# A sum of reciprocals on one core: the first load made in two transfers of 64 partitions

## The chip, the core and the metric

The kernel runs on one core of a Trainium2 chip. The metric is the device time of one execution in microseconds, as the median of several runs. Lower is better.

## What is computed

The input has 32 x 512 rows of 1024 values in float32, all positive. Of each row the kernel gives the sum of the reciprocals.

```python
def setup_inputs():
    batch, seq, dim = 32, 512, 1024
    return {
        "x": np.abs(np.random.randn(batch, seq, dim)).astype(np.float32) + 1e-6,
    }

def reference(x: np.ndarray) -> np.ndarray:
    return np.sum(1.0 / x, axis=-1).astype(np.float32)
```

The input is 64 MiB, the output 64 KiB. Each of the 128 partitions of on-chip memory gets 128 rows of the 16,384, and what the text calls "a row" is such a row on all partitions at once: 128 x 1024 values, 512 KiB.

## The kernel before

The rows pass through a ring of 40 places in on-chip memory. A plan, written out as a list of short words, gives the order of all operations. `D4 D8 D15 D13` at its start are loads of 4, 8, 15 and 13 rows, which fill the ring; the later loads, each smaller than these in the end, refill the places that have been used up.

The reciprocal is not taken directly. For the two halves a and b of a row, 1/a + 1/b = (a + b) / (ab). So the product ab is formed on GpSimd (`P`) or VectorE (`V`, `W`), ScalarE takes its logarithm (`L`) and the exponential of minus that (`E`), and VectorE multiplies and sums (`R`). The sum a + b comes from TensorE, as two matrix products with the identity that accumulate (`S`); in other rows VectorE multiplies both halves with 1/(ab) and sums. TensorE also copies halves of some rows into its accumulator memory for VectorE (`C`).

A load, a product on GpSimd and a copy on TensorE:

```python
            if op == "D":
                n, r = r, loaded
                while n:
                    q, at, w = place(r)
                    a = q % R
                    m = min(n, R - a, LAST - r) if r < LAST else 1
                    inst = nc.sync.dma_start(
                        out=ring[:, a : a + m, at : at + 2 * w],
                        in_=x_v[:, q : q + m, at : at + 2 * w],
                    )
                    note("SP", inst, writes=rows(r, m))
                    r, n = r + m, n - m
                loaded = r
            elif op == "P":
                # ... (cut)
                    inst = nc.gpsimd.tensor_tensor(
                        out=prod[:, p : p + m, :w],
                        in0=ring[:, a : a + m, at : at + w],
                        in1=ring[:, a : a + m, at + w : at + 2 * w],
                        op=mult,
                    )
                    note("POOL", inst, rows(r, m), slots(r, m))
                # ... (cut)
            elif op == "C":
                copied[r] = b
                inst = nc.tensor.matmul(
                    ps[:, b, : place(r)[2]],
                    lhsT=ident,
                    rhs=xs(r, 1),
                    start=True,
                    stop=True,
                )
                note("PE", inst, rows(r, 1, 1), [("bank", b)])
```

`x_v[:, q : q + m, ...]` has 128 partitions, and each partition's m rows lie one after the other in memory: four rows are 16 KiB in a piece.

`note` keeps account of what has read and written each place, and declares a dependency unneeded where another wait already implies it:

```python
    def note(engine, inst, reads=(), writes=()):
        # ... (cut: collects in `needed` the operations that this one must follow)
        for other in needed:
            o_inst, o_engine, o_tick, _, _, o_known = other
            if o_engine == engine:
                continue
            if o_tick <= known.get(o_engine, 0):
                tc.declare_no_dep(inst, o_inst, reason="implied by other waits")
                continue
            for e, t in o_known.items():
                known[e] = max(known.get(e, 0), t)
            known[o_engine] = max(known.get(o_engine, 0), o_tick)
        # ... (cut: a load is entered under a name of its own, "load 1", "load 2", ...)
```

Of the kernel before, what the change touches and what calls it, by code (L numbers as in the profile page):

```python
# [11 lines left out]
def kernel(  # L12
# [5 lines left out]
    nc = tc.nc  # L18
    f32 = mybir.dt.float32
    P = 128  # L20
# [58 lines left out]
    x_v = x.flatten_outer_dims().rearrange("(p f) d -> p f d", p=P)  # L79
# [16 lines left out]
    ring = pool.tile([P, R, D], f32)  # L96
# [15 lines left out]
    def place(r):  # L112
        if r < LAST:
            return r, 0, H
        part, q = divmod(r - LAST, F - LAST)
        return LAST + q, part * H, H // 2

    def xs(r, h):
        q, at, w = place(r)
        return ring[:, q % R, at + h * w : at + (h + 1) * w]  # L120

    loaded = 0
# [10 lines left out]
    def note(engine, inst, reads=(), writes=()):  # L133
        inst = inst.ins
        known = dict(begun.get(engine, {}))
        before = {}
        for spaces, writing in ((reads, False), (writes, True)):
            for space in spaces:
                for other in history.get(space, ()):
                    if writing or other[3]:  # L140
                        before[other[0].name] = other
        needed = sorted(before.values(), key=lambda o: -o[4])
# [4 lines that stand above are left out]
            if o_tick <= known.get(o_engine, 0):  # L147
                tc.declare_no_dep(inst, o_inst, reason="implied by other waits")
                continue
            for e, t in o_known.items():  # L150
                known[e] = max(known.get(e, 0), t)
            known[o_engine] = max(known.get(o_engine, 0), o_tick)
        count[engine] = count.get(engine, 0) + 1
        begun[engine] = known
        entry = (engine, count[engine])
        if engine == "SP":
            entry = (f"load {count[engine]}", 1)
        for spaces, writing in ((reads, False), (writes, True)):
            for space in spaces:
                history.setdefault(space, []).append(  # L160
                    (inst, *entry, writing, sum(count.values()), known)
                )

    def rows(r, n, h=None):
        spaces = []
        for q, at, w in (place(i) for i in range(r, r + n)):
            end = at + 2 * w
            if h is not None:
                at, end = at + h * w, at + (h + 1) * w
            spaces += [("row", q % R, i) for i in range(at, end, H // 2)]  # L170
        return spaces

    def slots(r, n):
        return [("slot", pslot[q]) for q in range(r, r + n)]

    with tc.manual_schedule():
        for op, r, n, b in ops:
            p = pslot.get(r)
# [3 lines that stand above are left out]
                    q, at, w = place(r)  # L182
                    a = q % R
                    m = min(n, R - a, LAST - r) if r < LAST else 1
                    inst = nc.sync.dma_start(  # L185
                        out=ring[:, a : a + m, at : at + 2 * w],
                        in_=x_v[:, q : q + m, at : at + 2 * w],
                    )
                    note("SP", inst, writes=rows(r, m))
                    r, n = r + m, n - m  # L190
                loaded = r
            elif op == "P":
                while n:
                    q, at, w = place(r)
                    a, p = q % R, pslot[r]
                    m = min(n, R - a)
# [18 lines that stand above are left out]
            elif op in "WV":  # L215
                w = place(r)[2]
                in1 = xs(r, 1) if op == "W" else ps[:, copied[r], :w]
                inst = nc.vector.tensor_tensor(  # L218
                    out=prod[:, p, :w], in0=xs(r, 0), in1=in1, op=mult
                )  # L220
                if op == "W":
                    read = rows(r, 1)
                else:
                    read = rows(r, 1, 0) + [("bank", copied[r])]
                note("DVE", inst, read, slots(r, 1))
            elif op == "S":
                bank[r] = b
                halves.add(r)
                for h in range(2):
# [3 lines that stand above are left out]
                        rhs=xs(r, h),  # L233
                        start=h == 0,
                        stop=h == 1,
                    )
                    note("PE", inst, rows(r, 1, h), [("bank", b)])
            elif op == "L":
                pg = prod[:, p : p + n, : place(r)[2]]
                inst = nc.scalar.activation(out=pg, in_=pg, func=Ln, scale=S)  # L240
                note("ACT", inst, writes=slots(r, n))
            elif op == "E":
                pg = prod[:, p : p + n, : place(r)[2]]
                rc = pg
                if b is not None:
                    rc = ps[:, b : b + n, : place(r)[2]]
                    for j in range(n):
                        bank[r + j] = b + j
                inst = nc.scalar.activation(out=rc, in_=pg, func=Exp, scale=-1.0)  # L249
                if b is None:  # L250
                    note("ACT", inst, writes=slots(r, n))
                else:
                    banks = [("bank", b + j) for j in range(n)]
                    note("ACT", inst, slots(r, n), banks)
            elif op == "R":
                q, at, w = place(r)
                other = ps[:, bank[r], :w]
                if r in halves:
                    row = prod[:, p, :w]
                else:  # L260
                    row = ring[:, q % R, at : at + 2 * w]
                    row = row.rearrange("p (h e) -> p h e", h=2)
                    other = other.unsqueeze(1).to_broadcast([P, 2, w])
                total = sums[:, q : q + 1]
                inst = nc.vector.tensor_tensor_reduce(  # L265
                    out=row,
                    in0=row,
                    in1=other,
                    scale=S,
                    scalar=total if q in summed else 0.0,  # L270
                    op0=mult,
                    op1=add,
                    accum_out=total,
                )
                summed.add(q)
                note(
                    "DVE",
                    inst,
                    [("bank", bank[r])],
                    slots(r, 1) if r in halves else rows(r, 1),  # L280
                )
        nc.sync.dma_start(out=out_v, in_=sums)
# [30 lines left out]
```

## Time and profile before

| | |
|---|---|
| time, median of 3 | 169.06 us (168.96 to 169.12) |
| span of the profiled execution | 167.1 us |
| read from HBM | 67.11 MB, 402 GB/s over the span |
| load queue | 94.8% of 16 DMA engines' span |
| busy: PE, DVE, ACT, POOL | 135.1, 128.2, 133.0, 128.0 us |
| the first load | 2048 KB; issued at 0.74 us, landed 7.3 us later |

The span is what the profiler saw from the first instruction to the last. PE is TensorE, DVE VectorE, ACT ScalarE, POOL GpSimd, and SP SyncE, which issues the loads. A line such as L197 is a line of the kernel. Where a group is listed with what "waited" before it, the arrow names the operation whose completion ended the wait. The DMA share is the mean busy share of the 16 DMA engines; it can exceed 1 in a short stretch, since a packet counts where it starts.

### The profile page before, as it was taken

Reading aid. Unit: us, or ns where it says so; the run is one execution under the profiler, and the core shown is the slowest. Engines: PE = TensorE matmul, PEld = TensorE weight load, DVE = VectorE, ACT = ScalarE, POOL = GpSimd, SP = SyncE. Lnnn points to the kernel's source line nnn. Section 1 sums busy time; section 2 is a strip of 40 time slices with the busy share of each in tenths; the row PEclk is TensorE's granted clock in tenths of the full one; section 3 lists DMA queues with packets and bytes.
Section 4 is the critical chain, followed back from the end, with each engine's and each line's share of the span. In section 5 each row is a group of like instructions: output and inputs, shape, how many; then the busy total and the mean of one; then the engine's idle time right before and its main releaser. Section 6 shows DMA issues by size and latency. Waiting matters only on the chain.

```text
span 167.1 us, 1335 instructions
## 1 busy us (share of the span) xinstructions
PE 135.1 (81%) x292; PEld 55.7 (33%) x292; DVE 128.2 (77%) x283; ACT 133.0 (80%) x161; POOL 128.0 (77%) x80
## 2 busy tenths in 40 slices
PE   0092799039999999977998999999699669989692
PEld 0030343023444334323333434434244133424261
DVE  0010298604789989886798898799999999999994
ACT  3045159207999999977999997999899999999992
POOL 1070792039999999939999997966899997979970
PEclk9999599965999999999999999999999999999999
DMA  5998999999999998999998989999999999999910
GB/s 192 435 502 377 471 471 471 471 408 408 408 408 407 439 466 377 441 424 439 412 471 384 479 377 447 416 449 412 422 428 429 405 432 408 428 408 409 396 64 16
DMA packets 4760, 67.26 MB, mean 403 GB/s; under 512 B 528, under 2 KB 656, under 8 KB 2192
## 3 DMA queue, kind: packets, MB, share of 16 engines
q1 hardware_dynamic: 4752, 67.18, 94.8%
q8 instruction: 2, 0.03, 0.1%
q14 instruction: 6, 0.05, 0.1%
HBM read 67.11 MB, written 0.07 MB: 402 GB/s over the span
## 4 chain that ended last, share of the span: by engine, by line
DMA 60%; DVE 16%; PE 15%; issue 3%; ACT 2%; SPq 1%; DVEq 0%; ACTq 0%
DMA ring<-in_x_dram 60%; PE ps L230 11%; DVE ring L265 10%; DVE prod L265 4%; PE ps L207 4%; DVE prod L218 2%; ACT prod L240 1%; DVE sums L265 1%; ACT prod L249 1%; ACT ps L249 1%; SPq L185 1%; DVEq L308 0%; ACTq L240 0%
## 5 line engine op out<-in xcount | busy, mean ns | idle before, releaser
L197 POOL TENSOR_TENSOR prod<-ring 128x1024 f32<-128x1024 f32 (+2 forms) x74 | 127.3, 1752 | 33.6 <-DMA ring<-in_x_dram 31.6
L230 PE MATMUL ps<-ring,ident 128*128 128x512 f32 (+1 forms) x260 | 118.6, 605 | 4.3 <-DVE sums L265 3.1
L240 ACT ACTIVATE prod<-prod 128x1024 f32<-128x1024 f32 (+2 forms) x80 | 69.0, 876 | 27.0 <-POOL prod L197 26.2
L265 DVE CUSTOM_DVE_ANT_1 ring<-ring,ps 128x1024 f32<-128x1024 f32 (+1 forms) x65 | 76.3, 1209 | 8.4 <-ACT ps L249 8.4
L230 PEld LDWEIGHTS ps<-ring,ident 128*128 128x128 f32 x260 | 49.8, 197 | 72.7 <-issue 51.7
L265 DVE CUSTOM_DVE_ANT_0 prod<-prod,ps 128x512 f32<-128x512 f32 (+1 forms) x63 | 40.7, 678 | 1.4 <-ACT prod L249 1.3
L207 PE MATMUL ps<-ring,ident 128*128 128x512 f32 x32 | 19.9, 712 | 24.5 <-DMA ring<-in_x_dram 24.5
L249 ACT ACTIVATE ps<-prod 128x1024 f32<-128x1024 f32 (+2 forms) x40 | 33.9, 854 | 2.5 <-DVE sums L265 1.8
L249 ACT ACTIVATE prod<-prod 128x1024 f32<-128x1024 f32 (+2 forms) x40 | 34.6, 874 | 0.8
L218 DVE TENSOR_TENSOR prod<-ring,ps 128x512 f32<-128x512 f32 x16 | 10.9, 685 | 26.6 <-PE ps L207 26.4
L207 PEld LDWEIGHTS ps<-ring,ident 128*128 128x128 f32 x32 | 5.9, 212 | 35.1 <-issue 16.3
L265 DVE DVE_READ_ACCUMULATOR2_ANT sums<- 128x1 f32 x130 | 10.7, 82 | 0.0
L218 DVE TENSOR_TENSOR prod<-ring 128x512 f32<-128x512 f32 (+1 forms) x7 | 4.5, 661 | 0.0
L83 ACT ACT_TABLE_LOAD x1 | 1.3, 1283 | 0.7 <-PEq L297 0.7
L265 DVE CUSTOM_DVE_ANT_0 prod<-prod,ps,sums 128x256 f32<-128x256 f32 x2 | 0.9, 478 | 0.0
masks.py:197 POOL MEMSET ident<- 128x128 f32 x1 | 0.2, 204 | 0.3 <-POOLq L297 0.3
masks.py:199 POOL TENSOR_SCALAR_AFFINE_SELECT ident<-ident 128x128 f32<-128x128 f32 x1 | 0.3, 292 | 0.1
L297 POOL MEMSET const-float32-0.0<- 128x1 f32 x1 | 0.1, 99 | 0.2 <-issue 0.2
L297 POOL MEMSET const-bfloat16-1.0<- 128x1 bf16 x1 | 0.1, 102 | 0.0
L297 POOL MEMSET const-uint8-127<- 128x1 uint8 x1 | 0.1, 102 | 0.0
L297 POOL MEMSET const-float32-1.0<- 128x1 f32 x1 | 0.1, 99 | 0.0
## 6 DMA issues: line engine op xcount, KB each, us to landing
ring<-in_x_dram SPq DMA_DIRECT2D x3, 4096.0 KB, 31.5
ring<-in_x_dram SPq DMA_DIRECT2D x4, 2048.0 KB, 34.4
ring<-in_x_dram SPq DMA_DIRECT2D x1, 7680.0 KB, 34.2
ring<-in_x_dram SPq DMA_DIRECT2D x2, 3584.0 KB, 32.3
ring<-in_x_dram SPq DMA_DIRECT2D x1, 6656.0 KB, 49.5
ring<-in_x_dram SPq DMA_DIRECT2D x2, 3072.0 KB, 32.6
ring<-in_x_dram SPq DMA_DIRECT2D x1, 5120.0 KB, 27.2
ring<-in_x_dram SPq DMA_DIRECT2D x4, 1024.0 KB, 30.3
```

The lines of the kernel that those rows point to most:

```text
L83: nc.scalar.add_instruction(mybir.InstLoadActFuncSet(name=nc.get_next_instruction_name(), act_func_set_id=act_sets.index("natural_log_exp_ ...
L185: inst = nc.sync.dma_start(out=ring[:, a : a + m, at : at + 2 * w], in_=x_v[:, q : q + m, at : at + 2 * w],)
L197: inst = nc.gpsimd.tensor_tensor(out=prod[:, p : p + m, :w], in0=ring[:, a : a + m, at : at + w], in1=ring[:, a : a + m, at + w : at + 2 * w],
L207: inst = nc.tensor.matmul(ps[:, b, : place(r)[2]], lhsT=ident, rhs=xs(r, 1), start=True, stop=True,)
L218: inst = nc.vector.tensor_tensor(out=prod[:, p, :w], in0=xs(r, 0), in1=in1, op=mult)
L230: inst = nc.tensor.matmul(ps[:, b, : place(r)[2]], lhsT=ident, rhs=xs(r, h), start=h == 0, stop=h == 1,)
L240: inst = nc.scalar.activation(out=pg, in_=pg, func=Ln, scale=S)
L249: inst = nc.scalar.activation(out=rc, in_=pg, func=Exp, scale=-1.0)
L265: inst = nc.vector.tensor_tensor_reduce(out=row, in0=row, in1=other, scale=S, scalar=total if q in summed else 0.0, op0=mult, op1=add, acc ...
L297: nc = _bacc.Bacc("TRN2", target_bir_lowering=False, num_devices=1)
```

## The change

The first load of four rows is made in two transfers. The first brings partitions 0 to 63, the second partitions 64 to 127. SyncE issues both, one after the other, and all later loads stay as they are. The aim is that the first bytes start to move after half as many descriptors have been prepared. The engines that use these rows wait for both transfers.

The second edit belongs to the first. Both transfers are entered as writers of the same rows, and without the edit the account would take the second for one that implies the first.

```diff
@@ note
             if o_tick <= known.get(o_engine, 0):
                 tc.declare_no_dep(inst, o_inst, reason="implied by other waits")
                 continue
+            if engine == "SP" and o_engine.startswith("load"):
+                continue
             for e, t in o_known.items():
                 known[e] = max(known.get(e, 0), t)
             known[o_engine] = max(known.get(o_engine, 0), o_tick)
@@ op == "D"
                     m = min(n, R - a, LAST - r) if r < LAST else 1
-                    inst = nc.sync.dma_start(
-                        out=ring[:, a : a + m, at : at + 2 * w],
-                        in_=x_v[:, q : q + m, at : at + 2 * w],
-                    )
-                    note("SP", inst, writes=rows(r, m))
+
+                    step = P if loaded else P // 2
+                    for p0 in range(0, P, step):
+                        inst = nc.sync.dma_start(
+                            out=ring[p0 : p0 + step, a : a + m, at : at + 2 * w],
+                            in_=x_v[p0 : p0 + step, q : q + m, at : at + 2 * w],
+                        )
+                        note("SP", inst, writes=rows(r, m))
                     r, n = r + m, n - m
```

## The prediction

> **What bounds the kernel now.** I read the page first: the busy shares by slice, the DMA queue line, the chain that ended last.
>
> ```profile
> DMA  5998999999999998999998989999999999999910
> ...
> q1 hardware_dynamic: 4752, 67.18, 94.8%
> ...
> DMA 60%; DVE 16%; PE 15%; issue 3%; ACT 2%; SPq 1%; DVEq 0%; ACTq 0%
> ```
>
> The first line is the share of the 16 DMA engines that is busy in each of 40 slices of 4.18 us: 5 in the first slice, then 9 or 8 up to the last two or three. The load queue q1 takes 94.8% of the span of 16 engines. 60% of the chain is loads. So the loads stream without a pause once they have begun. The view of stretches says it more exactly:
>
> ```profile
> core 0: us, PE busy (x) PEld busy (x) DVE busy (x) ACT busy (x) POOL busy (x), PEclk, DMA share, GB/s
> 0.00:4.00 4.00, 0.00 (x0) 0.00 (x0) 0.00 (x0) 1.28 (x1) 0.70 (x6) 1.00 0.55 184
> ...
> 8.00:40.00 32.00, 20.76 (x33) 8.29 (x34) 12.68 (x27) 14.03 (x18) 15.85 (x8) 0.86 1.02 440
> 40.00:80.00 40.00, 37.94 (x84) 15.39 (x83) 34.74 (x76) 36.50 (x37) 37.43 (x20) 0.98 0.99 424
> 80.00:120.00 40.00, 38.67 (x87) 15.56 (x85) 36.84 (x83) 37.88 (x43) 36.09 (x20) 1.00 1.00 429
> 120.00:152.00 32.00, 27.30 (x61) 11.28 (x62) 31.38 (x67) 31.57 (x43) 28.40 (x21) 1.00 1.00 418
> 152.00:158.00 6.00, 4.51 (x11) 1.76 (x10) 6.00 (x15) 5.86 (x11) 5.88 (x6) 1.00 1.03 403
> 158.00:162.00 4.00, 4.00 (x13) 2.10 (x12) 4.00 (x9) 3.86 (x8) 3.42 (x4) 1.00 0.36 134
> ```
>
> The last two columns are the DMA share and the rate. From 8 us to 158 us the share is 0.99 to 1.03: there is no slack in which lost DMA time could be made up. The compute engines are nearly as full in the second half (DVE 31.38 of 32 us), but they work on what the loads bring. So a delay at the front of the stream moves all that follows, loads and compute alike, by the same amount.
>
> Then the front itself. GpSimd's first products start when a load has landed:
>
> ```profile
> 8.12 3.57 POOL L197 TENSOR_TENSOR prod<-ring 128x1024 f32<-128x1024 f32 x2 [6.81 <-DMA ring<-in_x_dram]
> 17.81 2.34 POOL L197 TENSOR_TENSOR prod<-ring 128x1024 f32<-128x1024 f32 x1 [6.13 <-DMA ring<-in_x_dram]
> ```
>
> The first number is the start in us. The second load (eight rows, 4 MiB) lands about 17.81 - 8.12 = 9.69 us after the first (four rows, 2 MiB). 4,194,304 B / 9.69 us = 433 GB/s is the streaming rate here. At this rate 2 MiB take 4.84 us. The first load is issued at 0.74 us (timeline of SyncE), so 8.12 - 0.74 - 4.84 = 2.54 us is start and completion. Part of that start is uneven. The stretches of a quarter to half a microsecond at the beginning:
>
> ```profile
> 1.75:2.00 0.25, 0.00 (x0) 0.00 (x0) 0.00 (x0) 0.25 (x1) 0.00 (x0) 1.00 2.56 524
> 2.00:2.50 0.50, 0.00 (x0) 0.00 (x0) 0.00 (x0) 0.01 (x1) 0.00 (x0) 1.00 0.45 131
> 2.50:3.00 0.50, 0.00 (x0) 0.00 (x0) 0.00 (x0) 0.00 (x0) 0.00 (x0) 1.00 0.54 197
> 3.00:3.50 0.50, 0.00 (x0) 0.00 (x0) 0.00 (x0) 0.00 (x0) 0.00 (x0) 1.00 1.12 459
> ```
>
> A packet is counted in the stretch where it starts, so short stretches jump. 524 GB/s for 0.25 us is 131 KB, or eight packets of 16 KB (a partition's four rows). Then 131 and 197 GB/s for 0.5 us each are four and six more packets. So about eight engines have begun by 2.0 us, and the others come one by one over nearly a microsecond. That is the only idle time at the front that a quicker start could win: eight engines, some 0.5 us late on average, or a quarter of a microsecond of the whole.
>
> [...]
>
> [...] all transfers before have 128 partitions, and they stream at 433 GB/s. It can't show what 64 partitions do, as there is no such load in it. That is the open step of this prediction.
>
> **The change, part by part.**
>
> Removed: one load of 128 partitions by 16 KB, which takes 4.84 us of streaming.
>
> Added: two loads of 64 partitions by 16 KB. [...] each half streams at 433 / 2 = 216 GB/s: 1,048,576 B / 216 GB/s = 4.84 us each, 9.69 us for both. That is **+4.84 us** on the path that sets the end, since the second load queues behind it on the same engines.
>
> Given back: [...] From the uneven start above I take L at 0.2 to 0.3 us (my choice: the starts are spread over nearly 1 us, but in the stretch from 3.0 us on all engines are going): **-0.4 to -0.6 us**. [...] of the quarter of a microsecond above I count 0.1 us.
>
> SyncE issues one load more. The pieces of the chain show 0.38 and 0.42 us for such an issue. The second load's issue moves from about 1.2 to 1.6 us, while its turn on the engines doesn't come before 7 us: hidden, 0.
>
> Waits: TensorE's first copy and GpSimd's first product each wait for two completions instead of one. Both come to the same event, the later half[...].
>
> Bookkeeping: the program rotates eight completion counters over its loads (a load waits for the one eight places before it). With one more load in the row, a later load waits for what used to be seven places before. SyncE does wait there:
>
> ```profile
> SPq L185 <- DMA ring<-in_x_dram: 42.0, 15, 6.8
> ```
>
> But the queue is deep. The loads of one row (512 KB) land 15.0 us after issue and the last four (256 KB) 8.6 us, by the list of issues. One load fewer in flight takes 512 KB / 433 GB/s = 1.2 us or less off that, and the engines still have 7 us of work queued. So 0.
>
> The condition added to the dependency bookkeeping alone changes no work: the two halves may not count as one implying the other, so that both are waited for.
>
> Sum: 4.84 - 0.5 - 0.1 = about +4.2 us, or 173.3 us. First products at about 8.12 + 4.2 = 12.3 us.
>
> **The rivals.**
>
> (a) The engines follow the partition number [...]: the first half lands on eight engines with eight packets each, the second half on the other eight. [...] both halves run at once, and the time is 169.0 us within 0.3 us. For it: eight engines do begin first in this trace. [...] About 15%.
>
> (b) Half rate, but the engines drift apart far more than 0.3 us. [...] For it: the starts are spread over almost 1 us. Against it: at 3 us all engines are streaming. About 15%.
>
> (c) The aim of the change wins: the load starts earlier and nothing is lost. It can bring 0.25 us at most, by the stretches above, or 0.15%; a gain of over 2% (3.4 us) isn't to be had from a start that takes 2.54 us in all.
>
> (d) The loss comes at the front but is taken up later. This needs idle DMA time, and the share of 0.99 to 1.03 leaves none.
>
> **Range and chances.** The main case, two thirds, spreads from 3.4 to 4.9 us of loss. Case (b) lies between 1 and 3.4 us, and (a) with (c) at about 169. The 2% line is 3.38 us, at 172.4. I put the point a little under the sum, for (b): 173.1 us. The range from 169.0 to 174.2 takes in (a), since it costs most to miss. Slower by over 2%: 0.68; within 2%: 0.30; faster: 0.02.
>
> **What the profile after would show.** Step by step: the first two issues are 1 MiB each, and the rate between 3 us and 12 us is near 216 GB/s with the DMA share still near 1 (packets of 16 KB take about twice as long). GpSimd's first product starts near 12.3 us and its third near 22.0 us, still 9.7 us apart. From there all stretches look the same, 4.2 us later. If the first product starts near 8.1 us and the rate is 433 GB/s from the start, (a) is right. If it starts at 12.3 us and the end doesn't move as much, the step that the stream has no slack is wrong. The prediction fails most easily in the step the trace before can't show: that 64 partitions stream at half rate on this queue.

## The result and the profile after

The changed kernel takes 174.11 us (173.93 to 174.21, four runs) against 169.09 us (168.96 to 169.13, four runs) for the kernel before: a ratio of 1.0297, with a 95% interval of 1.0279 to 1.0315. The loss is 5.02 us.

The page of the changed kernel, its lines that answer to those shown of before:

```profile
DMA  5999999999999998999998999999999999999920
GB/s 129 232 247 411 442 457 457 457 457 396 396 396 429 448 468 362 451 407 435 441 472 381 472 419 400 430 457 436 407 424 426 403 431 411 424 407 411 398 84 15
...
q1 hardware_dynamic: 4768, 67.18, 94.9%
```

The first two lines belong together, slice by slice. The DMA engines are as busy as before, also in slices 2 and 3 (9 of 10), but there they move 232 and 247 GB/s instead of more than 400. A packet under way counts as busy however long it takes, so a busy share by itself doesn't show a lost rate; the line below it does. The queue holds 16 packets more than before (4768 against 4752), all of them under 512 B (544 against 528 on the pages): 16 for each of 34 transfers instead of 33, the completions of one more load.

The stretches at the front, in the changed kernel (the last two columns are DMA share and GB/s):

```profile
1.75:2.00 0.25, 0.00 (x0) 0.00 (x0) 0.00 (x0) 0.25 (x1) 0.00 (x0) 1.00 0.00 0
2.00:2.50 0.50, 0.00 (x0) 0.00 (x0) 0.00 (x0) 0.01 (x1) 0.00 (x0) 1.00 2.48 524
...
3.50:5.50 2.00, 0.00 (x0) 0.00 (x0) 0.00 (x0) 0.00 (x0) 0.00 (x0) 1.00 0.96 205
```

The last of these stretches in the kernel before:

```profile
3.50:5.50 2.00, 0.00 (x0) 0.00 (x0) 0.00 (x0) 0.00 (x0) 0.00 (x0) 1.00 0.96 410
```

Before, eight packets started between 1.75 and 2.00 us. Now none does, and then 524 GB/s for 0.5 us are 262 KB, or 16 packets: all 16 engines begin within half a microsecond (2.07 to 2.49 us), but on average 0.11 us later. From 3.5 to 5.5 us the rate is 205 GB/s, at the DMA share that goes with 410 GB/s before. In the trace a packet of 16 KB takes 1.28 us there (median), where it took 0.61 us before, and 16 such packets in 1.28 us are 205 GB/s too.

GpSimd's products, by which one sees the loads land:

```profile
13.45 3.57 POOL L202 TENSOR_TENSOR prod<-ring 128x1024 f32<-128x1024 f32 x2 [12.15 <-DMA ring<-in_x_dram]
22.89 8.24 POOL L202 TENSOR_TENSOR prod<-ring 128x1024 f32<-128x1024 f32 x4 [5.87 <-DMA ring<-in_x_dram]
```

The first load is there at 13.45 instead of 8.12 us, 5.33 us later. The second is 22.89 - 17.81 = 5.08 us later, and the span ends 172.2 - 167.1 = 5.1 us later. From the second load to the end nothing is made up and nothing is added. The last stretches show the same picture as before, moved by 5 us:

```profile
157.00:163.00 6.00, 4.51 (x11) 1.76 (x10) 6.00 (x15) 5.85 (x11) 5.88 (x6) 1.00 1.03 404
163.00:167.00 4.00, 4.00 (x12) 2.09 (x11) 4.00 (x9) 3.87 (x8) 3.40 (x4) 1.00 0.38 141
```

### The profile page after: what moved, and what is told of

Read it like the earlier page. It is cut to its first block, busy times and chain, and to the rows that moved or that the text cites. A ratio compares the mean times of both kernels' runs of the same rounds, so it can differ in the third digit from the quotient of the medians.

```text
span 172.2 us, 1338 instructions
## 1 busy us (share of the span) xinstructions
PE 135.1 (78%) x292; PEld 55.9 (32%) x292; DVE 128.3 (75%) x283; ACT 132.8 (77%) x161; POOL 128.0 (74%) x80
## 3 DMA queue, kind: packets, MB, share of 16 engines
q1 hardware_dynamic: 4768, 67.18, 94.9%
## 4 chain that ended last, share of the span: by engine, by line
DMA 46%; DVE 19%; issue 12%; POOL 12%; ACT 5%; PE 4%; SPq 1%; DVEq 0%; POOLq 0%
DMA ring<-in_x_dram 46%; DVE ring L270 13%; POOL prod L202 12%; DVE prod L270 3%; PE ps L235 3%; ACT prod L245 2%; DVE prod L223 2%; ACT ps L254 2%; PE ps L212 1%; DVE sums L270 1%; ACT prod L254 1%; SPq L190 1%; DVEq L313 0%; POOLq L202 0%
```

## The experiments

**Theory**: a transfer of partitions 0 to 63, or 64 to 127, streams at half rate, 205 GB/s where all 128 partitions have 410, and a stream without slack carries the loss to the end. What limits such a transfer is not shown by these traces. **Rivals**: one more transfer costs that much; 64 partitions are slow whatever they are; the start of the program is what is slow; it is the one queue that is slow. The time of the kernel before, on the chip of each group of runs, was between 168.97 and 169.08 us.

### Two transfers, split by rows

```diff
-                    step = P if loaded else P // 2
-                    for p0 in range(0, P, step):
+                    cut = m if loaded else m // 2
+                    for i in range(0, m, cut):
                         inst = nc.sync.dma_start(
-                            out=ring[p0 : p0 + step, a : a + m, at : at + 2 * w],
-                            in_=x_v[p0 : p0 + step, q : q + m, at : at + 2 * w],
+                            out=ring[:, a + i : a + i + cut, at : at + 2 * w],
+                            in_=x_v[:, q + i : q + i + cut, at : at + 2 * w],
                         )
-                        note("SP", inst, writes=rows(r, m))
+                        note("SP", inst, writes=rows(r + i, cut))
```

> The first load is again two transfers from SyncE, but split by rows: two rows each, all 128 partitions. [...] nothing is lost, 169.1 us within 0.3 us; the first products start earlier, near 5.8 us, and the stream stands where it stood before. Rival, the cost is that of one more transfer (issue, start, one completion counter fewer in rotation): 174 us, as the change.

Measured: 168.94 us, ratio 0.9995 (0.9987 to 1.0004). One more load, with its issue, its place among the completion counters and the edit in `note`, costs nothing. It brings nothing either, though the first products start 2.5 us earlier:

```profile
5.60 2.34 POOL L202 TENSOR_TENSOR prod<-ring 128x1024 f32<-128x1024 f32 x1 [4.30 <-DMA ring<-in_x_dram]
...
18.17 8.23 POOL L202 TENSOR_TENSOR prod<-ring 128x1024 f32<-128x1024 f32 x4 [8.51 <-DMA ring<-in_x_dram]
```

GpSimd then waits longer for the second load, which lands no earlier than before (18.17 against 17.81 us). Earlier compute at the front is worth nothing here. What an earlier stream would bring was not tried.

### Even and odd partitions

```diff
-                    step = P if loaded else P // 2
-                    for p0 in range(0, P, step):
+                    by = 1 if loaded else 2
+                    for p0 in range(by):
                         inst = nc.sync.dma_start(
-                            out=ring[p0 : p0 + step, a : a + m, at : at + 2 * w],
-                            in_=x_v[p0 : p0 + step, q : q + m, at : at + 2 * w],
+                            out=ring[p0:P:by, a : a + m, at : at + 2 * w],
+                            in_=x_v[p0:P:by, q : q + m, at : at + 2 * w],
                         )
```

> The first load in two transfers of 64 partitions each: 0, 2, 4 to 126, and then 1, 3, 5 to 127. [...] no loss, 169.1 to 169.5 us. [...] if each engine takes four neighbouring partitions of the list, say 0, 2, 4, 6 for the first[...]: 173.5 to 174.5 us, or 171 to 173 if the engines drift apart. Rival, 64 partitions are slow in themselves: 174.1 us.

Measured: 169.28 us, ratio 1.0014 (1.0007 to 1.0020). This is the change in every respect but one: two transfers of 64 partitions from SyncE, with the same bytes, packets and waits, and only the partitions of each are others. Its stretches:

```profile
1.75:2.00 0.25, 0.00 (x0) 0.00 (x0) 0.00 (x0) 0.25 (x1) 0.00 (x0) 1.00 0.00 0
2.00:2.50 0.50, 0.00 (x0) 0.00 (x0) 0.00 (x0) 0.01 (x1) 0.00 (x0) 1.00 1.43 360
...
3.50:5.50 2.00, 0.00 (x0) 0.00 (x0) 0.00 (x0) 0.00 (x0) 0.00 (x0) 1.00 1.03 434
```

434 GB/s from 3.5 us on, where the change has 205. So it isn't the number of partitions; it is which ones. I had held about half the rate possible here too (173.5 to 174.5 us), by the order of the packets; no trace showed a ground for that, and the 434 GB/s are against it. Why a half of the partitions is slow and every second one is not remains open: the trace doesn't tell which engine writes which partition. What is left of a loss, 0.2 us, fits the first line: no packet starts before 2 us, as in the change.

### A middle block and two outer ones

```diff
-                    step = P if loaded else P // 2
-                    for p0 in range(0, P, step):
+                    parts = [(0, P)] if loaded else [(32, 96), (0, 32), (96, P)]
+                    for p0, p1 in parts:
                         inst = nc.sync.dma_start(
-                            out=ring[p0 : p0 + step, a : a + m, at : at + 2 * w],
-                            in_=x_v[p0 : p0 + step, q : q + m, at : at + 2 * w],
+                            out=ring[p0:p1, a : a + m, at : at + 2 * w],
+                            in_=x_v[p0:p1, q : q + m, at : at + 2 * w],
                         )
```

> The first load in three transfers from SyncE: partitions 32 to 95, then 0 to 31, then 96 to 127. [...] the 64 partitions 32 to 95 lie in both halves and stream at the full 433 GB/s (1 MiB in 2.4 us, packets of 0.61 us), the two pieces of 32 partitions lie in one half each and stream at 205 GB/s (0.5 MiB in 2.6 us each). Together 7.5 us in place of 4.84, so 171.4 to 171.9 us, half the loss of the change. Rival, fewer than 128 partitions are slow in themselves: all 2 MiB at 205 GB/s, 174.1 us or more. Rival, each further transfer costs what the change did: 179 us.

Measured: 172.06 us, ratio 1.0177 (1.0160 to 1.0194), or +3.08 us; I had said 2.4 to 2.9. Both rates stand side by side in one kernel:

```profile
3.50:5.50 2.00, 0.00 (x0) 0.00 (x0) 0.00 (x0) 0.00 (x0) 0.00 (x0) 1.00 1.08 442
5.50:8.50 3.00, 0.00 (x0) 0.00 (x0) 0.00 (x0) 0.00 (x0) 0.00 (x0) 1.00 1.03 235
```

First the 64 partitions 32 to 95, which lie in both halves, at full rate (442 GB/s), then the outer blocks at about half (235 GB/s). The excess over the estimate fits a slow start: by the packet records the first 16 packets begin between 2.16 and 3.13 us, on average 0.60 us later than in the kernel before, and later than in any other of these kernels.

One rival is left. In `x_v` each partition has its own stretch of the input, so partitions 0 to 63 also read one half of the input in HBM, and 64 to 127 the other. The middle block reads as many stretches at the same spacing and runs at 442 GB/s, so neither of these is the reason. Whether each half of the input by itself can be read at half rate only was not tested; other rows in the same partitions would tell.

### Twelve rows instead of four

```diff
-                    step = P if loaded else P // 2
+                    step = P if loaded > 4 else P // 2
```

> The change, and the second load (eight rows, 4 MiB) is split into the two halves of the partitions too. A loss of rate grows with the bytes: three times 2 MiB at 205 instead of 433 GB/s, 3 x 5.3 less the 0.3 us that the change stayed below this, so about 184.6 us (183.5 to 185.5). A loss per further transfer: twice that of the change, 179.1 us. If the 7.1 us that the split in mid-run cost for 2 MiB come from the neighbours of the split load, the early loads here should stay near 5.3 us per 2 MiB; if every split load with a load ahead of it costs 7 us per 2 MiB, 188 us.

Measured: 184.35 us, ratio 1.0899 (1.0883 to 1.0916), or +15.3 us. Three times the bytes (6 MiB instead of 2) cost three times the time (15.3 us instead of 5.02).

```profile
13.39 3.57 POOL L202 TENSOR_TENSOR prod<-ring 128x1024 f32<-128x1024 f32 x2 [12.08 <-DMA ring<-in_x_dram]
33.57 4.67 POOL L202 TENSOR_TENSOR prod<-ring 128x1024 f32<-128x1024 f32 x2 [16.61 <-DMA ring<-in_x_dram]
```

The 4 MiB of the second load need 33.57 - 13.39 = 20.18 us, 4,194,304 B / 20.18 us = 208 GB/s, where they needed 9.69 us.

### The second half from ScalarE

```diff
                     for p0 in range(0, P, step):
-                        inst = nc.sync.dma_start(
+                        queue = nc.scalar if p0 else nc.sync
+                        inst = queue.dma_start(
```

> The halves of the change, the first from SyncE and the second from ScalarE's queue. If the 16 engines work through both queues in turn, and not all in the same half at the same time[...]: 169.0 to 171 us. If they go on in step, or finish one transfer before the other: 173.5 to 174.5 us. My guess is 172, with the second transfer begun about a microsecond later, behind ScalarE's table load.

Measured: 174.43 us, ratio 1.0319 (1.0300 to 1.0338), no better than one queue. My guess of 172 was wrong, and so was its reason: ScalarE issued its load at 0.76 us, beside its table load (0.73 to 2.01 us) and not behind it. Its packets (a queue of their own in the trace) still begin only at 6.5 us, when the last of the 64 packets of the first half has started (6.44 us), and then share the engines with the second load. The issues and their times to landing:

```profile
ring<-in_x_dram SPq DMA_DIRECT2D x1, 1024.0 KB, 9.0
ring<-in_x_dram ACTq DMA_DIRECT2D x1, 1024.0 KB, 16.6
```

The second half now lands 16.6 us after its issue, and GpSimd's first product waits until 17.52 us. Why the engines kept to the first queue for so long is not settled, and so two halves under way at the same time were not tested.

### The same split in mid-run

The first load is whole, and a load of four rows (rows 80 to 83, also 2 MiB) is split into the two halves.

```diff
-                    step = P if loaded else P // 2
+                    step = P // 2 if r == 80 else P
```

> The first load is whole again; a load of four rows in mid-run (rows 80 to 83, 2 MiB as well) is split into partitions 0 to 63 and 64 to 127. Theory that the stream has no slack and the loss is one of rate: 10.2 us for 2 MiB at 205 GB/s in place of 4.84, so +5.3 us or 174.4 us (174.0 to 174.6). Rival, the loss belongs to the start of the program: 169.1 us. Rival, the ring of 40 rows takes up a part in mid-run: 170 to 173 us.

Measured: 176.07 us, ratio 1.0430 (1.0394 to 1.0465), or +7.1 us. So the loss doesn't belong to the start of the program, and the ring takes up nothing of it. But it is 1.8 us more than the 5.3 I had worked out. The stretches from 99 to 113 us, first of this kernel (in its slowest execution, 177.17 us), then of the kernel before:

```profile
99.00:109.00 10.00, 8.56 (x21) 3.42 (x19) 6.75 (x16) 7.05 (x8) 7.06 (x4) 1.00 0.98 206
109.00:113.00 4.00, 1.02 (x3) 0.19 (x1) 2.99 (x8) 3.94 (x5) 3.09 (x2) 1.00 1.07 276
```

```profile
99.00:109.00 10.00, 9.89 (x24) 3.90 (x22) 8.68 (x20) 9.03 (x10) 9.13 (x5) 1.00 1.01 433
109.00:113.00 4.00, 4.00 (x10) 1.82 (x10) 4.00 (x10) 3.97 (x6) 2.17 (x2) 1.00 1.01 426
```

The low rate lasts until about 112 us, longer than 2 MiB at 206 GB/s (10.2 us) need. Packets of the load behind it, 24 KB each, take about 1.7 us until then instead of 0.91 in the kernel before. The neighbouring loads are slowed too.

### Where the extra loss in mid-run comes from

In mid-run the engines are no longer abreast. By the completion records of the kernel before, 16 to a load, which I read as one of each engine, they finish the load ahead of row 80 over 1.8 us, where they finish the first load over 0.5 us. Three more kernels bear on this: one with three pieces at the same place, and two with the split at places of different spread.

```diff
-                    step = P if loaded else P // 2
-                    for p0 in range(0, P, step):
+                    parts = [(32, 96), (0, 32), (96, P)] if r == 80 else [(0, P)]
+                    for p0, p1 in parts:
```

> The load of rows 80 to 83 in mid-run, split into partitions 32 to 95, 0 to 31 and 96 to 127. [...] 2.7 us at the bare rate, 3.5 us in proportion, so 171.7 to 172.6 us. If the extra loss in mid-run is that of a boundary between loads at which engines are 1 to 4 us apart, there are three such pieces and it stays: 173.5 to 174.5 us.

Measured: 173.41 us, ratio 1.0239 (1.0203 to 1.0275), or +4.3 us. This lies between the range in which half of the bytes have no loss, 171.7 to 172.6 us, and the other, and decides little; with half of the bytes in the middle block, 2.8 us of the 7.1 come back.

```diff
-                    step = P if loaded else P // 2
+                    step = P // 2 if r == 40 else P
```

> The fifth load (rows 40 to 46, 3.5 MiB) alone is split into partitions 0 to 63 and 64 to 127. In the kernel before, the 16 engines finish the load ahead of it within 0.47 us of each other (51.16 to 51.63 us). At 205 instead of 433 GB/s 3.5 MiB take 17.9 instead of 8.5 us: +9.4 us. If the extra 1.8 us of the split at row 80 come from engines that arrive at different times (1.8 us apart there), nearly none of it is here: 178.3 us (177.9 to 178.9). If any split load with whole loads around it has the extra, whatever the spread: 180.2 us (179.8 to 180.6).

Measured: 178.00 us, ratio 1.0514 (1.0437 to 1.0591), or +9.0 us for 3.5 MiB: 5.2 us for each 2 MiB, as at the front.

```diff
-                    step = P if loaded else P // 2
+                    step = P // 2 if r == 57 else P
```

> The seventh load (rows 57 to 63, 3.5 MiB as well) alone is split in the same way. In the kernel before, the engines finish the load ahead of it 1.85 us apart (71.78 to 73.63 us). Spread theory: +9.4 us and the extra of 1.8 us, 180.2 us (179.6 to 180.8), about 1.5 to 2 us above the split of the fifth load. Theory without the spread: the same as the split of the fifth load, within 0.4 us.

Measured: 179.55 us, ratio 1.0599 (1.0533 to 1.0666), or +10.6 us. The same edit on a load of the same size costs 1.55 us more where the engines arrive 1.85 us apart than where they arrive 0.47 us apart. The spread theory had said 1.5 to 2 us more; the time itself lies 0.05 us below its range. It remains a comparison of two places: the spread itself was not set, and how engines that arrive apart lose time is not shown.

None of these kernels is measurably faster than the one before.

## Why the prediction was right

**The open step**, that 64 partitions of one half stream at half rate: right. In the kernel before no load has 64 partitions, so its trace gave no ground for the half; it is now shown for partitions 0 to 63 and 64 to 127, at 205 to 208 GB/s against 433, with the even and odd partitions as the control (434 GB/s), and the middle block 32 to 95 as a second one (442 GB/s). Where the limit sits is not shown: the traces hold rates and not their cause, and the rival of the halves of the input stands.

**No slack in the stream**: right. Delays of 5.08 us at the second load and 5.1 us at the end of the span agree.

**One issue more, waits, counters**: right, nothing, as the split by rows shows too (168.94 us). SyncE's waits for earlier loads are what they were, in spite of the shifted counters:

```profile
SPq L190 <- DMA ring<-in_x_dram: 42.0, 15, 6.9
```

**Rival (a)**, engines that follow the partition number: refuted by 16 packets that begin within 0.42 us and by 205 GB/s. **Rival (b)**, a loss cut by engines far apart: not seen. By the completion records the engines finish the first half 0.82 us apart, and a quarter of a microsecond at most came back. **Rivals (c) and (d)**: refuted, by the result and by the split in mid-run.

**The sum was 0.8 us too small**, 4.2 against 5.02. Three of its terms were mis-sized:

- The rate. I took exactly half, 9.69 us for 2 MiB. At 208 GB/s they take 10.09 us: 0.40 us more.
- What I thought given back by uneven starts, 0.5 us: twice the lead L of some engines over others, which no trace showed. The second load lands 22.89 - 13.45 = 9.44 us after the first instead of 9.69: 0.25 us at most came back. The step from uneven starts to a lead did not hold: in the kernel before, the eight packets that start first take 1.1 to 1.4 us and the other eight 0.7 to 1.0 us, so all 16 end between 2.93 and 3.44 us. In mid-run, too, engines further apart went with a larger loss, not a smaller one.
- The quicker start, 0.1 us. SyncE's first issue takes 0.558 us instead of 0.381, and the engines begin between 2.07 and 2.49 us instead of 1.76 and 2.66: more evenly, but on average 0.11 us later. The gain was a loss of 0.11 us.

4.84 + 0.40 - 0.25 + 0.11 = 5.10 us, beside the measured 5.02. The first products at 13.45 instead of the predicted 12.3 us show the same error.

The half rate without slack was right, but that the range held was close: 174.11 us lies 0.09 us below its upper end, and the loss of 5.02 us is more than the 3.4 to 4.9 us of the main case. The width of the range lay on the other side, for rival (a). The aim of the change failed in its own step too: 64 packets per transfer instead of 128 did not make the first packet start earlier in any kernel that begins with 64 partitions (2.07 to 2.16 us in five of them, 1.75 to 1.76 us in the six that begin with 128).

## What to carry to other kernels

When a load is to be split, split it along the free dimension and keep all 128 partitions (168.94 us here, against 168.98 for the whole load); if it must be split by partitions, take every second one (169.28 us) rather than halves (174.11 us), and measure. In a stream that keeps all DMA engines busy from first to last, as here, the time lost by one load was paid in full at the end wherever it was tried (for halves 5.02 us at the front, 7.1 to 10.6 us in mid-run), while compute that started 2.5 us earlier gained nothing. Read the DMA share together with the GB/s below it: engines whose packets took 1.28 us instead of 0.61 had the same share, 0.96, at 205 instead of 410 GB/s.

## What was not expected

The first load of 64 partitions took longer to issue on SyncE than the first one of 128: 0.558 against 0.381 us. The three whole loads behind the halves took 0.51 to 0.58 us as well, where they took 0.42, 0.42 and 0.72 us before. And the rate of the halves is less than half, 205 to 208 GB/s against 433: a packet of 16 KB took 1.28 us, not twice 0.61. In mid-run, a split into halves cost 7.1 us for 2 MiB instead of 5 us, and the packets of the loads around it were slower as well.
